# Rotary embedding, eight rows on one core: homes as separate buffers, and one row's load alternating with another's store

## The chip, the cores and the metric

The kernel runs on one core of a Trainium2 chip. The metric is the device time of one execution in microseconds (us). Before the change the median of three runs is 316.32 us (316.31 to 316.72).

## The reference

The input `x` has 8 batch rows of 2048 positions, 16 heads and 64 numbers, all fp32. Each pair of neighbouring numbers is rotated by the angle of its position and of its place in the head:

```python
x_pairs = x.reshape(batch, seq_len, num_heads, head_dim // 2, 2)
x1 = x_pairs[..., 0]
x2 = x_pairs[..., 1]
...
out1 = x1 * cos - x2 * sin
out2 = x1 * sin + x2 * cos
out = np.stack([out1, out2], axis=-1).reshape(batch, seq_len, num_heads, head_dim)
```

`cos` and `sin` have a row of 32 numbers for each position and are the same for all batch rows and heads. 67.1 MB come in and 67.1 MB go out.

## The kernel before

A "row" is one of the eight batch rows, 8.39 MB in fp32. It is laid over the 128 partitions with 16 neighbouring positions on each, so that a partition holds 16 x 1024 = 16384 numbers: 64 KB in fp32 in memory, one contiguous run, and 32 KB in bf16 on chip. Loads that POOL issues convert fp32 to bf16 on their way in, and its stores convert back. A DMA of a whole row is 128 such runs, eight for each of the 16 DMA engines. All loads and stores that POOL issues go through one queue (q0 in the profile) and are taken in the order of issue; SP issues two DMAs through a queue of its own (q1).

There is room for five rows in bf16. The buffer `xt` has five homes, and `HOME` gives row b its home: rows 0 to 4 have homes 0 to 4, and rows 5, 6 and 7 take homes 0, 1 and 2 once rows 0, 1 and 2 are stored.

`rotate(b)` does the work of a row in place with three VectorE (DVE) instructions of 128 x 16384 numbers: L89 multiplies the row by the sine table into `qt`, L92 multiplies the row by the cosine table, and L97 adds `qt`, read with each pair's two numbers swapped. The tables `s_tab` and `c_tab` are built once, the sine with alternating sign (L110 to L112).

The order is written out by hand, and on each engine the instructions run in that order:

- SP loads the first quarter of row 0 in fp32 (`head`, L101) and ACT casts it into its home (L108). POOL issues the loads of the two tables (L102, L103), of the rest of row 0 (L104), of rows 1 and 2 in one DMA, and of rows 3 and 4 in one DMA (`load`, L70).
- DVE builds the tables and rotates row 0 in two parts (4 and 12 positions of 16), then rows 1 to 7.
- `first_store` runs between the first and the second instruction of row 2's rotation. Two one-element copies on ACT, the first of which reads `qt` (L120, L121), hold the store of row 0 (`store`, L74) until that instruction is done.
- Before the store of rows 1 and 2, POOL copies one element of row 4's home into `mark` (L126), so that the store is issued only when rows 3 and 4 have landed.
- Then POOL issues the store of rows 1 and 2 in one DMA, the load of row 5 (which waits for the store of row 0), the load of rows 6 and 7 in one DMA (which waits for the store of rows 1 and 2), the store of rows 3 and 4, and the store of rows 5 and 6, each waiting for its rotations.
- Row 7 leaves in another way. ACT casts it in four parts to fp32 into `wide` (L138), which is the space of homes 3 and 4, and SP stores it (L139).

A DMA is put into its queue when its instruction's waits are over; each DMA posts its completion with a small packet on each engine.

Of the kernel before, what the change touches and what calls it, by code (L numbers as in the profile page):

```python
# [2 lines left out]

# [4 lines left out]


@with_exitstack  # L10
def kernel(
    ctx: ExitStack,
    tc: tile.TileContext,
    x: bass.AP,
    cos: bass.AP,
    sin: bass.AP,
    out: bass.AP,
):
    nc = tc.nc
    fp32 = mybir.dt.float32  # L20
    bf16 = mybir.dt.bfloat16
    mult = mybir.AluOpType.mult
    add = mybir.AluOpType.add

    B, S, H, D = x.shape
    P = 128
    K = S // P
    KP = 16
    D2 = D // 2
    HD = H * D  # L30
    NX = 5
    HEAD = 4
    PART = 4
    STAGE = 3


    HOME = [0, 1, 2, 3, 4, 0, 1, 2]

    x_t = x.rearrange("b (p k) h d -> b p k (h d)", p=P, k=K)
    out_t = out.rearrange("b (p k) h d -> b p k (h d)", p=P, k=K)  # L40
    x_r = x.rearrange("b (p k) h d -> p b (k h d)", p=P, k=K)
    out_r = out.rearrange("b (p k) h d -> p b (k h d)", p=P, k=K)
    cos_t = cos.rearrange("(p k) c -> p (k c)", p=P, k=K)
    sin_t = sin.rearrange("(p k) c -> p (k c)", p=P, k=K)

    consts = ctx.enter_context(tc.tile_pool(name="consts", bufs=1))
    stage = ctx.enter_context(tc.tile_pool(name="stage", bufs=1))

    xt = consts.tile([P, NX, K * HD], bf16)
    cos_sb = consts.tile([P, K * D2], fp32)  # L50
    sin_sb = consts.tile([P, K * D2], fp32)
    c_tab = consts.tile([P, K, D], bf16)
    s_tab = consts.tile([P, K, D], bf16)

    wide = (
        xt[:, STAGE : STAGE + 2]
        .rearrange("p a c -> p (a c)")
        .bitcast(fp32)
        .rearrange("p (k c) -> p k c", c=HD)
    )  # L60

    gate = consts.tile([1, 1], bf16)
    mark = consts.tile([1, 1], bf16)

    def home(b, k0=0, k1=K):
        return xt[:, HOME[b], k0 * HD : k1 * HD].rearrange("p (k c) -> p k c", c=HD)

    def load(b, n):
        h = HOME[b]
        nc.gpsimd.dma_start(out=xt[:, h : h + n], in_=x_r[:, b : b + n])  # L70

    def store(b, n):
        h = HOME[b]
        nc.gpsimd.dma_start(out=out_r[:, b : b + n], in_=xt[:, h : h + n])  # L74

    def rotate(b, k0=0, k1=K, between=None):
        nk = k1 - k0
        xp = home(b, k0, k1)
        qt = stage.tile([P, KP, HD], bf16, name="qt", tag="work")

        def rows(a):
            return a.rearrange("p k (h e) -> p k h e", h=H, e=D)

        def tab(a):
            return dataclasses.replace(
                a, offset=a.offset + k0 * D, ap=[a.ap[0], [D, nk], [0, H], [1, D]]
            )

        nc.vector.tensor_tensor(out=rows(qt[:, :nk]), in0=rows(xp), in1=tab(s_tab), op=mult)  # L89
        if between is not None:  # L90
            between(qt)
        nc.vector.tensor_tensor(out=rows(xp), in0=rows(xp), in1=tab(c_tab), op=mult)  # L92
        q_swap = dataclasses.replace(
            qt, offset=qt.offset + 1, ap=[qt.ap[0], [2, nk * HD // 2], [-1, 2]]
        )
        x3 = xp.rearrange("p k (a j) -> p (k a) j", j=2)
        nc.vector.tensor_tensor(out=x3, in0=x3, in1=q_swap, op=add)  # L97

    with tc.manual_schedule():
        head = stage.tile([P, HEAD, HD], fp32, name="st", tag="work")  # L100
        nc.sync.dma_start(out=head[:, :HEAD], in_=x_t[0, :, :HEAD])  # L101
        nc.gpsimd.dma_start(out=sin_sb, in_=sin_t)  # L102
        nc.gpsimd.dma_start(out=cos_sb, in_=cos_t)  # L103
        nc.gpsimd.dma_start(out=home(0, HEAD), in_=x_t[0, :, HEAD:])  # L104
        load(1, 2)
        load(3, 2)

        nc.scalar.copy(out=home(0, 0, HEAD), in_=head[:, :HEAD])  # L108
        s2 = s_tab.rearrange("p k (i j) -> p (k i) j", j=2)
        nc.vector.tensor_copy(out=s2[:, :, 0], in_=sin_sb)  # L110
        nc.vector.tensor_scalar_mul(s2[:, :, 1], sin_sb, -1.0)  # L111
        nc.vector.tensor_copy(  # L112
            out=c_tab.rearrange("p k (i j) -> p (k i) j", j=2),
            in_=cos_sb.to_broadcast([P, K * D2, 2]),
        )
        rotate(0, 0, HEAD)
        rotate(0, HEAD, K)

        def first_store(qt):
            nc.scalar.copy(out=gate, in_=qt[:1, KP - 1, HD - 1 :])  # L120
            nc.scalar.copy(out=xt[:1, HOME[0], :1], in_=xt[:1, HOME[0], :1])  # L121
            store(0, 1)

        rotate(1)
        rotate(2, between=first_store)
        nc.gpsimd.tensor_copy(out=mark, in_=xt[:1, 4, K * HD - 1 :])  # L126
        store(1, 2)
        load(5, 1)
        load(6, 2)
        rotate(3)  # L130
        rotate(4)
        store(3, 2)
        for b in range(5, B):
            rotate(b)
            if b == 6:
                store(5, 2)
        for k in range(0, K, PART):
            nc.scalar.copy(out=wide[:, k : k + PART], in_=home(B - 1, k, k + PART))  # L138
        nc.sync.dma_start(out=out_t[B - 1], in_=wide)  # L139


# [1 line left out]
_INS = ['x', 'cos', 'sin']  # L143
_OUTS = [((8, 2048, 16, 64), 'float32')]


# [23 lines left out]
```

## Time and profile before

| | us |
|---|---|
| median of the runs | 316.32 |
| the profiled execution's own time | 316.21 |
| its span, first to last instruction | 314.4 |
| DVE busy (30 instructions) | 210.4 |
| DVE idle ahead of L89 | 49.3 |
| ACT busy | 19.3 |
| POOL busy | 12.4 |
| HBM read and written, 67.63 + 67.11 MB | 429 GB/s over the span |

The profile is of one execution. A full row's rotation is three DVE instructions of 8.69 us with gaps of 0.03, 26.15 us together. In the page's second part each digit is the busy share of one of 40 equal slices of the span, in tenths, and its GB/s counts the bytes on the side that is written, so that a load to bf16 counts half of what it reads. DMA times "to landing" run from the issue to the completion. In the chain of waits "another core or an unknown queue" is a wait whose end the profile couldn't put down to an instruction; here these pieces end when a row has landed.

### The profile page before, as it was taken

The numbers are of one execution on the slowest core, as the hardware profiler recorded it, in microseconds if no ns is written. First come the engines' busy times: TensorE is split into PE (matmuls) and PEld (weight loads), VectorE is DVE, ScalarE is ACT, GpSimd is POOL, SyncE is SP. The second block draws the span as 40 slices with busy tenths as digits, with TensorE's granted clock in tenths as the row PEclk, the third lists the DMA queues.
The fourth block names the chain that finished last, engine by engine and source line by source line (L and its number), as shares of the span: only waits on it lengthen the run. The fifth ranks groups of instructions, "written<-read, shape, count | busy, mean of one in ns | idle before, by whom it ended". The sixth has DMA issues, their size and how long they took to land.

```text
span 314.4 us, 114 instructions
## 1 busy us (share of the span) xinstructions
DVE 210.4 (67%) x30; ACT 19.3 (6%) x8; POOL 12.4 (4%) x16
## 2 busy tenths in 40 slices
DVE  0549950099999999999992299903999999200000
ACT  1400000000000000000000000000000000790000
POOL 4000000000002500000000000000000000000000
DMA  7999999999999999999999999999999999999996
GB/s 296 238 267 200 200 200 267 200 200 217 250 200 267 459 475 400 400 492 442 400 200 246 221 200 200 250 217 333 400 525 409 400 400 525 409 400 400 525 409 267
DMA packets 2512, 102.24 MB, mean 325 GB/s; under 512 B 208, under 2 KB 208, under 8 KB 336
## 3 DMA queue, kind: packets, MB, share of 16 engines
q0 software_dynamic: 2224, 91.75, 92.0%
q1 hardware_dynamic: 288, 10.49, 7.9%
HBM read 67.63 MB, written 67.11 MB: 429 GB/s over the span
## 4 chain that ended last, share of the span: by engine, by line
DVE 64%; another core or an unknown queue 13%; DMA 7%; ACT 3%; ACTq 1%; issue 0%; POOL 0%; DVEq 0%; PEldq 0%
DVE qt L89 21%; DVE xt L92 21%; DVE xt L97 21%; DMA xt<-in_x_dram 7%; ACT xt L138 3%; ACTq L165 1%; POOL sin_sb L102 0%; POOL cos_sb L103 0%; DVEq L89 0%; DVEq L92 0%; PEldq L165 0%
## 5 line engine op out<-in xcount | busy, mean ns | idle before, releaser
L89 DVE TENSOR_TENSOR qt<-xt,s_tab 128x16384 bf16<-128x16384 bf16 (+2 forms) x9 | 69.7, 7744 | 49.3 <-DMA xt<-in_x_dram 47.0
L92 DVE TENSOR_TENSOR xt<-xt,c_tab 128x16384 bf16<-128x16384 bf16 (+2 forms) x9 | 69.7, 7743 | 0.4
L97 DVE TENSOR_TENSOR xt<-xt,qt 128x16384 bf16<-128x16384 bf16 (+2 forms) x9 | 69.7, 7744 | 0.3
L138 ACT CAST xt<-xt 128x4096 f32<-128x4096 bf16 x4 | 14.1, 3600 | 171.7 <-DVE xt L97 171.7
L74 POOL DMA_DIRECT2D out_dram<-xt x4 | 2.7, 672 | 184.9 <-ACT xt L121 93.5
L110 DVE CAST s_tab<-sin_sb 128x512 bf16<-128x512 f32 x1 | 0.5, 456 | 8.9 <-DMA sin_sb<-in_sin_dram 8.9
L120 ACT COPY gate<-qt 1x1 bf16<-1x1 bf16 x1 | 0.2, 194 | 85.1 <-DVE qt L89 85.1
L126 POOL COPY mark<-xt 1x1 bf16<-1x1 bf16 x1 | 5.0, 5040 | 2.6 <-DMA xt<-in_x_dram 2.6
L70 POOL DMA_DIRECT2D xt<-in_x_dram x4 | 2.7, 694 | 43.2 <-DMA out_dram<-xt 43.2
L108 ACT CAST xt<-st 128x4096 bf16<-128x4096 f32 x1 | 3.6, 3605 | 6.7 <-DMA st<-in_x_dram 6.7
L108 ACT ACT_TABLE_LOAD x1 | 1.3, 1283 | 0.7 <-PEq L154 0.7
L102 POOL DMA_DIRECT2D sin_sb<-in_sin_dram x1 | 0.7, 696 | 0.8 <-PEq L165 0.8
L112 DVE CAST c_tab<-cos_sb 128x1024 bf16<-128x1024 f32 x1 | 0.7, 685 | 0.0
L103 POOL DMA_DIRECT2D cos_sb<-in_cos_dram x1 | 0.6, 569 | 0.0
L104 POOL DMA_DIRECT2D xt<-in_x_dram x1 | 0.6, 557 | 0.0
L111 DVE TENSOR_SCALAR s_tab<-sin_sb 128x512 bf16<-128x512 f32 x1 | 0.4, 445 | 0.0
L121 ACT COPY xt<-xt 1x1 bf16<-1x1 bf16 x1 | 0.2, 188 | 0.0
L154 POOL MEMSET const-float32-0.0<- 128x1 f32 x1 | 0.1, 99 | 0.2 <-issue 0.2
L154 POOL MEMSET const-bfloat16-1.0<- 128x1 bf16 x1 | 0.1, 103 | 0.0
L154 POOL MEMSET const-float32-1.0<- 128x1 f32 x1 | 0.1, 99 | 0.0
L154 POOL MEMSET const-uint8-127<- 128x1 uint8 x1 | 0.1, 99 | 0.0
## 6 DMA issues: line engine op xcount, KB each, us to landing
xt<-in_x_dram POOLq DMA_DIRECT2D x3, 8192.0 KB, 59.4
xt<-in_x_dram POOLq DMA_DIRECT2D x1, 4096.0 KB, 57.6
xt<-in_x_dram POOLq DMA_DIRECT2D x1, 3072.0 KB, 21.2
st<-in_x_dram SPq DMA_DIRECT2D x1, 2048.0 KB, 8.0
sin_sb<-in_sin_dram POOLq DMA_DIRECT2D x1, 256.0 KB, 7.6
cos_sb<-in_cos_dram POOLq DMA_DIRECT2D x1, 256.0 KB, 7.4
out_dram<-xt POOLq DMA_DIRECT2D x4, 49.8
out_dram<-xt SPq DMA_DIRECT2D x1, 30.0
```

The lines of the kernel that those rows point to most:

```text
L70: nc.gpsimd.dma_start(out=xt[:, h : h + n], in_=x_r[:, b : b + n])
L74: nc.gpsimd.dma_start(out=out_r[:, b : b + n], in_=xt[:, h : h + n])
L89: nc.vector.tensor_tensor(out=rows(qt[:, :nk]), in0=rows(xp), in1=tab(s_tab), op=mult)
L92: nc.vector.tensor_tensor(out=rows(xp), in0=rows(xp), in1=tab(c_tab), op=mult)
L97: nc.vector.tensor_tensor(out=x3, in0=x3, in1=q_swap, op=add)
L102: nc.gpsimd.dma_start(out=sin_sb, in_=sin_t)
L103: nc.gpsimd.dma_start(out=cos_sb, in_=cos_t)
L108: nc.scalar.copy(out=home(0, 0, HEAD), in_=head[:, :HEAD])
L112: nc.vector.tensor_copy(out=c_tab.rearrange("p k (i j) -> p (k i) j", j=2), in_=cos_sb.to_broadcast([P, K * D2, 2]),)
L126: nc.gpsimd.tensor_copy(out=mark, in_=xt[:1, 4, K * HD - 1 :])
L138: nc.scalar.copy(out=wide[:, k : k + PART], in_=home(B - 1, k, k + PART))
L165: with _tile.TileContext(nc) as tc:
```

## The change

The one buffer `xt` becomes four: homes 0, 1 and 2 have one each, and homes 3 and 4 stay together, since `wide` lies over both. `at(b)` gives a row's buffer and its place there. The load of rows 1 and 2 becomes two DMAs, and so do the stores of rows 1 and 2, 3 and 4, and 5 and 6, and the load of rows 6 and 7. The copy into `mark` is left out.

`load` and `store` can take every eighth partition. The load of row 6 and the store of row 3 are each cut into eight DMAs of 16 partitions, g, g + 8, ... g + 120, and POOL issues them in turn: a load, a store, a load, a store. The load of row 7 and the store of row 4 follow. The stores of rows 5 and 6 each come after their own rotation. VectorE, ACT and SP run the same instructions as before, on the new buffers.

```diff
-    xt = consts.tile([P, NX, K * HD], bf16)
+    homes = [consts.tile([P, n, K * HD], bf16, name=f"x{i}") for i, n in enumerate((1, 1, 1, 2))]
...
-        xt[:, STAGE : STAGE + 2]
+        homes[3][:, :2]
...
-    mark = consts.tile([1, 1], bf16)
...
-        return xt[:, HOME[b], k0 * HD : k1 * HD].rearrange("p (k c) -> p k c", c=HD)
+        t, h = at(b)
+        return t[:, h, k0 * HD : k1 * HD].rearrange("p (k c) -> p k c", c=HD)
 
-    def load(b, n):
-        h = HOME[b]
-        nc.gpsimd.dma_start(out=xt[:, h : h + n], in_=x_r[:, b : b + n])
+    def at(b):
+        return homes[min(HOME[b], 3)], max(HOME[b] - 3, 0)
 
-    def store(b, n):
-        h = HOME[b]
-        nc.gpsimd.dma_start(out=out_r[:, b : b + n], in_=xt[:, h : h + n])
+    def load(b, n, g=0, step=1):
+        t, h = at(b)
+        nc.gpsimd.dma_start(out=t[g::step, h : h + n], in_=x_r[g::step, b : b + n])
+
+    def store(b, n, g=0, step=1):
+        t, h = at(b)
+        nc.gpsimd.dma_start(out=out_r[g::step, b : b + n], in_=t[g::step, h : h + n])
...
-        load(1, 2)
+        load(1, 1)
+        load(2, 1)
         load(3, 2)
...
         rotate(1)
         rotate(2, between=first_store)
-        nc.gpsimd.tensor_copy(out=mark, in_=xt[:1, 4, K * HD - 1 :])
-        store(1, 2)
+        store(1, 1)
+        store(2, 1)
         load(5, 1)
-        load(6, 2)
         rotate(3)
         rotate(4)
-        store(3, 2)
+        for g in range(G):
+            load(6, 1, g, G)
+            store(3, 1, g, G)
+        load(7, 1)
+        store(4, 1)
         for b in range(5, B):
             rotate(b)
-            if b == 6:
-                store(5, 2)
+            if b < B - 1:
+                store(b, 1)
```

More of the change, by code (lines that the diff above doesn't have):

```diff
@@ L120, in first_store @@
             nc.scalar.copy(out=gate, in_=qt[:1, KP - 1, HD - 1 :])
-            nc.scalar.copy(out=xt[:1, HOME[0], :1], in_=xt[:1, HOME[0], :1])
+            nc.scalar.copy(out=homes[0][:1, 0, :1], in_=homes[0][:1, 0, :1])
             store(0, 1)
```

3 lines of the change are left out of this document (1 added, 2 removed).

## The prediction

> **What bounds the kernel now.** I read the chain of waits first, because it tempts one to the wrong answer:
>
> ```profile
> DVE 64%; another core or an unknown queue 13%; DMA 7%; ACT 3%; ACTq 1%; issue 0%; POOL 0%; DVEq 0%; PEldq 0%
> ```
>
> VectorE has 64% of the chain, so it looks like the bound. The rows on DMA say otherwise:
>
> ```profile
> DMA  7999999999999999999999999999999999999996
> ...
> q0 software_dynamic: 2224, 91.75, 92.0%
> q1 hardware_dynamic: 288, 10.49, 7.9%
> ```
>
> The two queues' packets fill 99.9% of the time of all 16 DMA engines, and only the first and last of 40 slices are below 9. So the end is the sum of the packets: every store and load stands in one line, and VectorE's idle times are waits for its row's turn in that line. The issues show it again: the last store takes 30 us to land, though a row needs only 19.3 (next paragraph), since it shares the engines with the store of rows 5 and 6.
>
> ```profile
> out_dram<-xt SPq DMA_DIRECT2D x1, 30.0
> ```
>
> The timeline gives the price of a row:
>
> ```profile
> 98.02 0.56 POOL L74 DMA_DIRECT2D out_dram<-xt  x1 [93.53 <-ACT xt L121]
> 101.13 5.04 POOL L126 COPY mark<-xt 1x1 bf16<-1x1 bf16 x1 [2.55 <-DMA xt<-in_x_dram]
> ...
> 120.76 0.58 POOL L70 DMA_DIRECT2D xt<-in_x_dram  x1 [4.90 <-DMA out_dram<-xt]
> ...
> 178.49 8.69 DVE L89 TENSOR_TENSOR qt<-xt,s_tab 128x16384 bf16<-128x16384 bf16 x1 [11.15 <-DMA xt<-in_x_dram]
> ...
> 217.05 8.69 DVE L89 TENSOR_TENSOR qt<-xt,s_tab 128x16384 bf16<-128x16384 bf16 x1 [12.41 <-DMA xt<-in_x_dram]
> ```
>
> Row 5 has landed at 178.5 and rows 6 and 7 at 217.05: 38.6 us for two rows, 16 packets on each engine, 2.412 us a packet. Store 0 runs from 101.1 (loads 3 and 4 landed) to 120.8: 19.6 us for eight packets with POOL's wake-up. Load and store cost the same, 64 KB of fp32 in 2.412 us on each engine (27.2 GB/s), whichever side the fp32 is on.
>
> Does a load overlap a store where they meet now? The DMA view of the stretch from 155 to 163 us, in slices of 0.2 us, counts bytes where packets start:
>
> ```profile
> GB/s 0 0 0 983 2621 1311 328 0 0 0 0 0 0 0 0 0 1639 819 164 0 0 0 0 0 0 0 0 0 1638 819 164 0 0 0 0 0 0 0 0 0
> ```
>
> The last round of store 1-2 starts at 155.77, the first of load 5 at 158.22, the second at 160.63 (first starts, from narrower windows): 4.86 us for a store round and a load round, where two rounds of one kind take 4.825. So nothing is gained at the border, and 0.04 is lost. Read in the same way, load then store (213.73 to 218.56) loses 0.00, load then load across two DMAs (175.11 to 179.95) 0.02, store then store (117.16 to 122.00) 0.02.
>
> **The change, part by part.** Homes as buffers of their own change no size and no DVE instruction (nine rotations, 210.4 us in all).
>
> Load 1-2 in two DMAs: row 1 can be rotated when it lands, at 62.4 - 19.3 = 43.1, not at 62.4; row 0 ends at 43.6, so the idle 18.95 us before row 1 goes and DVE runs some 19 us earlier. Store 0 is then issued near 79. Nothing is gained: the line holds loads until 101, and store 0 still starts there. Should that cover be gone, the 19 us would count. Price: one border load-load, 0.02, and an issue of 0.7 us on POOL behind 90 us of queued loads.
>
> The mark copy goes (5.04 us of POOL). It delayed store 1-2, which stood behind store 0 in the line anyway: 0. Store 1-2 in two DMAs: one border, 0.02; load 5 still waits for store 0, to 120.8, while stores 1 and 2 fill the line to 159.
>
> The interleave. In the program each DMA of the POOL queue takes one of eight semaphores in turn, so from the seventh of the sixteen on each waits for the DMA eight before it, and load 7, store 4, store 5 and store 6 are queued behind these waits on POOL. The first three pairs can be issued from 140 (store 1 landed), the fourth load when store 2 lands (159) and its store when load 5 does (178). From there seven packets, 17 us, always stand ahead of an issue of 0.6 us, so the line doesn't run dry. If that cover were gone, each issue would show about 2.3 us, as between the issue of store 0 (98.02) and its first packet (100.29). The line carries the same bytes, but with a border at each packet: 8 load-store borders at 0.00 and 8 store-load ones (the last before load 7) at 0.04 make 0.32. Store 5 | store 6 adds 0.02; load 7 | store 4 and store 4 | store 5 replace borders that are there now.
>
> Row 6 lands one packet before the interleave's end, about 215 (now 217), row 7 near 236. DVE ends row 7 at 215 + 2 x 26.15 = 267, ACT's four casts (14.1) end at 281, and the last store is issued 2 us earlier than its 283.55. The line is full with stores 4 to 6 until 294, so this is worth 0, and up to some 10 us of delay there would be too.
>
> What the trace doesn't show is a DMA whose 16 rows lie eight partitions apart. If two engines then share a way into SBUF, it must carry 2 x 32 KB in 2.412 us, 27.2 GB/s. Lower end: it does, 0. (A gain is excluded by the engines' own 2.412 us unless load and store overlap, which is a rival.) Upper end: the pair takes turns, 16 x 2.412 = 38.6 us. Nearest row: the head's load, fp32 on both sides, starts 16 KB packets 0.62 us apart, 26.4 GB/s into SBUF; at that rate a pair takes 2.48 us, 16 x 0.068 = 1.1 us more. Part of that is the gap of a small packet, so I take half, 0.55. [...]
>
> Sum: 0.02 + 0.02 + 0.32 + 0.02 = 0.38, with 0.55 it is 0.93. The profiled execution took 316.21 (span 314.4, the rest around it is not touched): 317.14. It lies 0.11 under the median of 316.32, so against the median 317.25; I say 317.2.
>
> **The rivals.** *Overlap (faster).* The change would pay if an engine could read for the next packet while it writes this one. A load and a store together move 96 KB each way, 3.62 us at 27.2 GB/s instead of 4.825; eight pairs save 9.65 us: 316.3 + 0.4 - 9.65 = 307.1. For it: loads fill only the read side, stores only the write side. Against it: the store-load and load-store borders above gained nothing, and those in the interleave are the same event, each with the completion's packet between.
>
> *Eight engines (the change doesn't do what it says).* If packets follow the partition, pairs 0 to 3 fall on eight engines, two packets each, and 4 to 7 on the others. With eight DMAs outstanding the second set starts only when the first load is done: 178.0 + 4.8 + 2.3 = 185.1, 7.1 us late, and ends so: 323.8. For it: eight rows of every whole-row DMA belong to an engine; against it: nothing in the trace.
>
> *Starved issues.* If POOL can build descriptors only between DVE's 8.69 us instructions, then during row 5's rotation (178.5 to 204.6) one DMA gets in at 187.2 and one at 195.9; with the seven standing at 178.0 they last to 199.7, and the next packet comes 2.3 us after 204.6: 7.2 us lost, 323.9. For it: the mark copy was held 5.04 us, to the end of the DVE instruction (106.13). Against it: store 0 was issued at 98.02, inside that same instruction, and ran from 101 on. [...]
>
> *Ways taken in turn*: 316.7 + 38.6 = 355.3. For it: each pair would need all of a way; against it: where engines fall out of step, one loads while the other stores.
>
> **How the numbers follow.** The forecast, borders plus a nearly full way, spans 316.7 (0) to 317.8 (1.1) and gets 0.60; eight engines 0.10, starved issues 0.08, turns 0.07, overlap 0.15. A measurement tells 0.2%, 0.63 us, from no change, so the bound on the slow side is 316.95: of the forecast 0.27 lies under it and 0.33 over it. Slower 0.33 + 0.25 = 0.58, within 0.27, faster 0.15. The range runs from 315.6 (a trace of overlap; 0.13 of it left out) to 324.0 (both 7 us rivals in; turns left out, 0.07).
>
> **What would show it.** Right: both queues still near 100% of the engines; row 1 rotated from 43.6 and store 0 issued near 79; in the stretch from 178 to 217 rounds of packets 2.41 to 2.45 us apart, alternately 32 and 64 KB. Overlap: rounds nearer 1.8 us, row 7 landing near 227. Shared ways: rounds of 2.48 or longer there alone, with longer packets. Eight engines: rounds of eight packets. Starved issues: a gap in the DMA row between 195 and 207. I am wrong altogether if the time moves where the line isn't touched, ahead of 178 or after 236.

## The result, and the profile after

The changed kernel takes 317.59 us (median of 7 runs, 317.27 to 317.82) against 316.32 before (median of 7 runs, 316.27 to 317.29): 1.27 us more. The ratio is 1.0037, with a 95% interval of 1.0027 to 1.0046. The profiled execution took 317.49 us with a span of 315.7, where the one before had 316.21 and 314.4.

From the page of the changed kernel, the DMA row, the queues, and the shares of the chain of waits:

```profile
DMA  7999999999999999999999999999999999999996
...
q0 software_dynamic: 2528, 91.75, 92.1%
q1 hardware_dynamic: 288, 10.49, 7.9%
...
DVE 56%; DMA 24%; ACT 3%; another core or an unknown queue 3%; POOL 1%; ACTq 1%; issue 1%; DVEq 0%; PEldq 0%
```

The two queues fill the 16 engines as before, so the line of packets is still the bound. There are 304 small completion packets more, 19 DMAs of 16. The chain has less of VectorE and more of the load, and this too says nothing of the bound: only the place where DVE waits has moved.

The timeline of the changed kernel at the steps that the prediction named:

```profile
43.45 8.69 DVE L91 TENSOR_TENSOR qt<-x,s_tab 128x16384 bf16<-128x16384 bf16 x1
...
78.94 1.10 POOL L76 DMA_DIRECT2D out_dram<-x  x2 [74.12 <-ACT x L124]
...
121.95 0.53 POOL L72 DMA_DIRECT2D x<-in_x_dram  x1 [25.35 <-DMA out_dram<-x]
...
215.97 8.69 DVE L91 TENSOR_TENSOR qt<-x,s_tab 128x16384 bf16<-128x16384 bf16 x1 [10.43 <-DMA x<-in_x_dram]
...
282.48 0.35 SPq L145 DMA_DIRECT2D out_dram<-x  x1
```

Row 1's rotation and store 0's issue are where they were expected (43.6, near 79). Row 5's load, which waits for store 0, is issued 1.2 us later than before (120.76), and that is ahead of the interleave. So the packets were read in rounds, much as for the prediction. A round is one packet on each of the 16 engines, and it begins here with the first start in it, that of a completion packet ahead of it included. A border is the place where the packets of one DMA follow those of another:

| stretch, in rounds of 16 packets | before, us | after, us | more |
|---|---|---|---|
| start to the first packet of row 1 | 23.02 | 22.92 | -0.10 |
| loads 1 and 2, 16 rounds | 38.63 | 38.65 | 0.02 |
| loads 3 and 4, first 15 rounds | 36.21 | 36.28 | 0.07 |
| loads 3 and 4, last round | 2.41 | 3.36 | 0.95 |
| stores 0 to 2, 24 rounds | 57.91 | 57.93 | 0.02 |
| load 5, 8 rounds | 19.34 | 19.34 | 0.00 |
| next 16 rounds (after: the interleave) | 38.63 | 38.91 | 0.28 |
| last 40 rounds, to the last completion | 96.56 | 96.65 | 0.08 |

The sum is 1.32; the spans differ by 1.3. Two of these lines as the window view has them (length, DVE, ACT and POOL busy, PE clock, DMA share, GB/s on the written side), first before, then after (in the kernel after, the rounds begin 0.04 us later than these windows and have the same length):

```profile
177.52:216.15 38.63, 26.08 (x3) 0.00 (x0) 0.00 (x0) 1.00 1.01 217
97.86:100.27 2.41, 2.41 (x1) 0.00 (x0) 0.56 (x1) 1.00 0.95 204
```

```profile
178.44:217.35 38.91, 27.45 (x4) 0.00 (x0) 6.01 (x12) 1.00 1.01 323
97.81:101.17 3.36, 0.00 (x0) 0.00 (x0) 0.00 (x0) 1.00 1.02 156
```

The 16 rounds of the interleave cost 0.28 us more than 16 rounds of loads. (Their GB/s are higher only because a store's bytes are counted in fp32.) The trace shows what stands at its borders: on each engine a completion packet of 4 bytes, which takes 0.022 us behind a load and 0.042 behind a store that a load follows.

The largest piece, 0.95 us, lies in one round of plain loads, the last before the first store, 77 us ahead of the interleave: the engines are shown busy all through it, and it moves its 0.52 MB at 156 GB/s, where plain loads have 204 to 217. Each of its 16 packets is itself longer, 3.27 to 3.65 us against 2.43 to 2.45 in the kernel before, so this isn't a gap between packets. That piece wasn't in the prediction.

### The profile page after: what moved, and what is told of

It reads as the page before. It is cut to its first block, busy times and chain, and to the rows that moved or that the text cites. A ratio compares the mean times of both kernels' runs of the same rounds, so it can differ in the third digit from the quotient of the medians.

```text
span 315.7 us, 139 instructions
## 1 busy us (share of the span) xinstructions
DVE 210.4 (67%) x30; ACT 19.3 (6%) x8; POOL 15.9 (5%) x34
## 4 chain that ended last, share of the span: by engine, by line
DVE 56%; DMA 24%; ACT 3%; another core or an unknown queue 3%; POOL 1%; ACTq 1%; issue 1%; DVEq 0%; PEldq 0%
DMA x<-in_x_dram 24%; DVE qt L91 19%; DVE x L94 19%; DVE x L99 19%; ACT x L144 3%; ACTq L171 1%; POOL out_dram L76 0%; POOL x L72 0%; POOL sin_sb L104 0%; POOL cos_sb L105 0%; DVEq L91 0%; PEldq L171 0%
## 5 line engine op out<-in xcount | busy, mean ns | idle before, releaser
L91 DVE TENSOR_TENSOR qt<-x,s_tab 128x16384 bf16<-128x16384 bf16 (+2 forms) x9 | 69.7, 7745 | 48.5 <-DMA x<-in_x_dram 46.3
L99 DVE TENSOR_TENSOR x<-x,qt 128x16384 bf16<-128x16384 bf16 (+2 forms) x9 | 69.7, 7743 | 0.3
L94 DVE TENSOR_TENSOR x<-x,c_tab 128x16384 bf16<-128x16384 bf16 (+2 forms) x9 | 69.7, 7743 | 0.3
L144 ACT CAST x<-x 128x4096 f32<-128x4096 bf16 x4 | 14.1, 3602 | 189.7 <-DVE x L99 189.7
L76 POOL DMA_DIRECT2D out_dram<-x x14 | 7.2, 516 | 168.9 <-ACT x L124 74.1
L72 POOL DMA_DIRECT2D x<-in_x_dram x13 | 6.9, 536 | 57.1 <-DMA out_dram<-x 47.0
L111 ACT CAST x<-st 128x4096 bf16<-128x4096 f32 x1 | 3.6, 3605 | 6.5 <-DMA st<-in_x_dram 6.5
L106 POOL DMA_DIRECT2D x<-in_x_dram x1 | 0.6, 556 | 0.0
```

The lines of the kernel that those rows point to most:

```text
L72: nc.gpsimd.dma_start(out=t[g::step, h : h + n], in_=x_r[g::step, b : b + n])
L76: nc.gpsimd.dma_start(out=out_r[g::step, b : b + n], in_=t[g::step, h : h + n])
```

## The experiments

Times are medians; the kernel before, run beside each on the same chip, took 316.28 to 316.42.

**Whole rows again.** To part the interleave from the rest, row 6's load and row 3's store go back to one DMA each.

```diff
-        for g in range(G):
-            load(6, 1, g, G)
-            store(3, 1, g, G)
+        load(6, 1)
+        store(3, 1)
```

> The changed kernel with row 6's load and row 3's store each in one DMA of 128 partitions again, in this order; all else as changed. Theory (the early stores cost about 1.0 us at the first border of loads and stores, near 98 us, and the interleave only its 0.34 us of borders): 317.2, and the round of packets that starts near 97.8 again lasts about 3.4 us. Rival (the interleave is what costs, the long round at 98 us is chance): 316.4.

317.33 us, ratio 1.0028 (1.0017 to 1.0040): 1.02 more than before without any interleave, and the round at 97.82 lasts 3.66 us in its profile. The interleave isn't the main cost.

**Store 0 issued later.** The first of the two ACT copies that hold the store reads the end of row 2's home after its rotation, instead of `qt` after its first instruction.

```diff
-        def first_store(qt):
-            nc.scalar.copy(out=gate, in_=qt[:1, KP - 1, HD - 1 :])
+        def first_store():
+            nc.scalar.copy(out=gate, in_=homes[2][:1, 0, K * HD - 1 :])
...
-        rotate(2, between=first_store)
+        rotate(2)
+        first_store()
```

> The changed kernel with row 0's store held until row 2's rotation is done, so that it is issued near 96 instead of 79 us, 5 us ahead of the first border instead of 22. Theory (a store that stands in the queue long ahead of the border costs): 316.7, and the round at 98 us lasts 2.41 us. Rival one (any store issued ahead of the last load's round costs): 317.6. Rival two (the early stores have nothing to do with it): 317.6 with the long round.

317.43 us, ratio 1.0035 (1.0023 to 1.0047). Store 0 is issued at 96.7, and the packets of the round at 97.86 still take 2.75 to 3.38 us, 3.20 on average. The theory that it takes a long stand in the queue falls: being issued 1.1 us ahead of the last load's round is enough.

**The kernel before with an early store.** One word is moved.

```diff
-        rotate(1)
-        rotate(2, between=first_store)
+        rotate(1, between=first_store)
+        rotate(2)
```

> The kernel before with row 0's store held only by the first instruction of row 1's rotation, so that it is issued near 72 us instead of 98; nothing else is changed, and there is no interleave. Theory (early issue costs): 317.2 to 317.4, with a long round near 98 us. Rival (early issue costs nothing, since the store starts at 101 us in either case): 316.3.

317.25 us, ratio 1.0028 (1.0018 to 1.0039). The early issue alone makes the loss, in the old kernel with its one buffer, its mark and its double loads. The timeline and then the window view of this run:

```profile
71.97 0.55 POOL L74 DMA_DIRECT2D out_dram<-xt  x1 [67.48 <-ACT xt L121]
```

```profile
98.05:101.37 3.32, 3.32 (x1) 0.00 (x0) 0.00 (x0) 1.00 1.00 158
```

The last load round takes 3.32 us, and DVE is busy all through it, so an idle DVE (as in the changed kernel) isn't the reason either.

**The interleave alone.** Rows 1 and 2 share a buffer again, with one load, one store and the mark; row 0's store is issued at 97.9.

```diff
-    homes = [consts.tile([P, n, K * HD], bf16, name=f"x{i}") for i, n in enumerate((1, 1, 1, 2))]
+    homes = [consts.tile([P, n, K * HD], bf16, name=f"x{i}") for i, n in enumerate((1, 2, 2))]
...
-        load(1, 1)
-        load(2, 1)
+        load(1, 2)
...
-        store(1, 1)
-        store(2, 1)
+        nc.gpsimd.tensor_copy(out=mark, in_=homes[2][:1, 1, K * HD - 1 :])
+        store(1, 2)
```

> The changed kernel with rows 1 and 2 in one buffer, loaded in one DMA and stored in one, and the mark copy back: up to row 5's load everything is issued as in the kernel before, and then comes the interleave. Theory (the interleave costs eight borders of 0.04 us): 316.7 (316.32 plus 0.32 for the interleave and 0.02 for one more border), no round longer than 2.46 us between 178 and 220 us. Rival (half of the ways into SBUF, nearly full, cost up to 1.1 us): 317.2 to 317.8, with rounds of 2.48 us.

316.58 us, 0.27 more than before (ratio 1.0006, 0.9998 to 1.0015). That fits the borders, 0.34, and not the 1.1 of a nearly full way.

**The first store moved between the loads.** If the slow round belongs to the first border from loads to stores, it must move with it. The two copies that hold the store, and the mark, are left out.

```diff
         load(1, 2)
-        load(3, 2)
...
+        store(0, 1)
+        load(3, 2)
...
-        rotate(2, between=first_store)
-        nc.gpsimd.tensor_copy(out=mark, in_=xt[:1, 4, K * HD - 1 :])
+        rotate(2)
```

> The kernel before with row 0's store issued between the load of rows 1-2 and that of rows 3-4 (near 44 us, some 18 us ahead of its border), without the two gate copies and the mark; no interleave. Theory one (the first border from loads to stores is slow when its store is already queued): the round of packets ahead of the border at 62 us lasts about 3.4 us, none does near 120 us, and the time is 317.3. Theory two (any such border is slow that has a store queued for long): long rounds at 62 and at 120 us, 318.2. Rival (it hangs on row 4's load or on the time near 98 us): no long round at 62 us, 316.3.

317.43 us, ratio 1.0033 (1.0020 to 1.0045). The DMA view of this run in slices of 0.25 us, from 57 and then from 116 us, shows rounds of loads and then of stores where they start:

```profile
GB/s 1442 131 0 0 0 0 0 0 0 1311 655 131 0 0 0 0 0 0 0 0 0 0 0 262 2884 1049 0 0 0 0 0 0 0 1311 2884 0 0 0 0 0
...
GB/s 918 1180 0 0 0 0 0 0 0 131 1180 786 0 0 0 0 0 0 0 786 2884 524 0 0 0 0 0 0 0 2097 2097 0 0 0 0 0 0 0 524 2621
```

In the first line the last load round starts in the 10th slice and the first store round only 14 slices on (59.30 to 62.96, 3.65 us). In the second line, at the next border from loads to stores, whose store was queued early too, the rounds stay ten slices apart. So the slow round is neither tied to row 4 nor to 98 us, and it comes once.

**A small store first, on SP and on POOL.** Two runs look for what "first" means.

```diff
+        nc.sync.dma_start(out=out_t[0, :KP, 0, : K * D2], in_=sin_sb[:KP])
```

> The changed kernel with a small store added on SP (16 partitions of 2 KB, one for each engine, from the sine table's buffer into output row 0, which row 0's store writes over later), near 9 us. Theory one (what is slow is the core's first write to the output or first read of the chip's memory by a DMA): no long round at 98 us, 316.7 to 316.8. Rival (a store queued behind the loads slows the last of them, whatever has been written earlier): the long round stays, 317.6 to 317.7.

317.76 us, ratio 1.0040 (1.0026 to 1.0054), and the round at 98.22 lasts 3.3 us. An engine's first write to the output isn't it.

```diff
+    first = consts.tile([KP, 512], bf16)
...
+        nc.gpsimd.dma_start(out=out_r[:KP, 0, :512], in_=first)
         load(1, 1)
```

> The changed kernel with a small bf16-to-fp32 store on POOL's queue (16 partitions of 2 KB fp32, zeros that row 0's store writes over) between row 0's load and row 1's. Theory one (the long round belongs to the first store of POOL's queue, once a run): no long round at 98 us, one near 21 to 23 us instead, 317.6. Theory two (it belongs to the first whole-row store behind loads): the long round stays at 98 us, 317.7, and none near 22.

317.67 us, ratio 1.0038 (1.0026 to 1.0051). The DMA view of this run from 95 us:

```profile
GB/s 0 0 1442 524 131 0 0 0 0 0 0 262 1442 393 0 0 0 0 0 0 0 0 0 0 262 1049 2622 262 0 0 0 0 0 0 786 2621 786 0 0 0
```

The last load round starts in the 12th slice and the first store round in the 25th, 3.27 us on: the long round stays, though each engine has carried a store of POOL's queue with the same conversion, of 2 KB.

**One full packet first.** Here an eighth of row 0, one 64 KB packet on each engine, is stored between the loads, and the whole row later.

```diff
         load(2, 1)
-        load(3, 2)
...
         rotate(0, HEAD, K)
+        store(0, 1, 0, G)
+        load(3, 2)
```

> The changed kernel with one sixteenth-partition piece of row 0 (16 partitions, one 64 KB packet for each engine) stored already between the load of row 2 and that of rows 3-4; the whole of row 0 is stored later as before, so that 2.41 us of packets are added: 317.6 + 2.4 = 320.0. Theory (the first full packet that an engine stores is slow to come when it stands ready behind loads, and only that one): a round of 3.4 us ahead of 62 us, none near 101 us. Rival (it takes a whole row's store, or it hangs on the time since the start): no long round at 62 us, one near 103 us.

320.01 us, ratio 1.0107 (1.0089 to 1.0125), with 2.41 us of it in the added packets. The DMA view of this run from 57 and from 98 us:

```profile
GB/s 1573 393 131 0 0 0 0 0 0 131 1704 262 0 0 0 0 0 0 0 0 0 0 0 1049 2359 786 0 0 0 0 0 0 0 787 1049 262 0 0 0 0
...
GB/s 0 0 0 0 655 1180 262 0 0 0 0 0 0 131 1049 918 0 0 0 0 0 0 0 1049 1835 1311 0 0 0 0 0 0 0 1311 2359 524 0 0 0 0
```

The round of loads ahead of the single packet takes 3.36 us (59.49 to 62.85). Ahead of the whole row's store, issued at 79.2 and so again early, the rounds stay 2.41 us apart (the last load round starts at 101.50, the first store round at 103.91). One full packet on each engine is enough to have paid. It isn't shown that its size is what counts: the 2 KB stores also lay in the first 1 MB of the output, and these packets are spread over all of row 0.

**The changed kernel with store 0 at 98.** One element of row 2 is copied on DVE ahead of row 1's rotation, so that DVE waits as it did before the change.

```diff
+    mark = consts.tile([1, 1], bf16)
...
+        nc.vector.tensor_copy(out=mark, in_=homes[2][:1, 0, K * HD - 1 :])
         rotate(1)
```

> The changed kernel with one element of row 2's home copied on DVE ahead of row 1's rotation, so that DVE waits for row 2 as it did before the change and row 0's store is issued near 98 us again; loads, stores and interleave as changed. Theory (of the change's 1.27 us about 0.95 is the early store and the rest borders): 316.7, no round of 3.4 us near 98. Rival (the separate loads or the missing mark cost, not the time of the store's issue): 317.5.

316.59 us, 0.31 more than before (ratio 1.0008, 0.9999 to 1.0017). The timeline and then the window view of this run:

```profile
98.04 1.10 POOL L77 DMA_DIRECT2D out_dram<-x  x2 [93.21 <-ACT x L125]
```

```profile
97.81:100.25 2.44, 2.44 (x1) 0.00 (x0) 1.10 (x2) 1.00 1.00 215
```

The store is issued 0.2 us into the last load's round, and the round takes 2.44. Holding DVE back by 19 us, and with it the store, makes the changed kernel 1.0 us faster.

**Neighbouring partitions.** The interleave of the fourth run, with partitions 16g to 16g + 15 in a DMA.

```diff
-        nc.gpsimd.dma_start(out=t[g::step, h : h + n], in_=x_r[g::step, b : b + n])
+        nc.gpsimd.dma_start(out=t[g : g + step, h : h + n], in_=x_r[g : g + step, b : b + n])
...
-            load(6, 1, g, G)
-            store(3, 1, g, G)
+            load(6, 1, g * KP, KP)
+            store(3, 1, g * KP, KP)
```

> The interleave on the order of the kernel before, as in the earlier run of it (316.58), with each of the sixteen DMAs on 16 neighbouring partitions instead of every eighth. [...] If engines don't share ways, rounds of 2.43 us and 316.6.

331.34 us, ratio 1.0473 (1.0458 to 1.0487). The window view of the interleave in this run:

```profile
177.52:230.60 53.08, 26.60 (x4) 0.00 (x0) 6.00 (x12) 1.00 1.03 246
```

16 rounds take 53.1 us instead of 38.9, 3.32 us each with the engines shown busy all the time. So DMAs of 16 neighbouring partitions take 1.4 times as long, and the change's choice of every eighth partition avoids that. That shared ways into SBUF are the cause is the author's guess and not shown: with the partitions the edit also changes the places in memory, 1 MB in a row for each DMA instead of 16 pieces half a MB apart, and no run parts the two. The trace shows 16 x 16 x 32 KB in 53.08 us, 158 GB/s over both directions; in the first round, which is loads alone, the packets took 3.58 us on average, 146 GB/s.

**The interleave doubled.** On the fourth run, row 7's load and row 4's store alternate too.

```diff
-        load(7, 1)
-        store(4, 1)
+        for g in range(G):
+            load(7, 1, g, G)
+            store(4, 1, g, G)
```

> The interleave on the order of the kernel before (316.58), and row 7's load and row 4's store alternating in the same way too, 8 and 8 DMAs more. Theory (the interleave costs its store-load borders, 0.04 us each): 316.58 + 8 x 0.04 = 316.9. Rival (load and store overlap when they alternate for long, hidden by other losses so far): below 316.3.

344.23 us, ratio 1.0880 (1.0865 to 1.0895), far from both. The window view and the timeline of this run:

```profile
177.78:255.60 77.82, 27.54 (x4) 0.00 (x0) 12.71 (x26) 1.00 1.01 323
```

```profile
254.13 8.69 DVE L93 TENSOR_TENSOR qt<-x,s_tab 128x16384 bf16<-128x16384 bf16 x1 [49.35 <-DMA x<-in_x_dram]
```

The 32 rounds take 77.8 us, 2.43 each, as the border theory has it. But row 6's rotation, whose row was in by 217, starts only when row 7's last piece has landed: in this kernel rows 6 and 7 are in one buffer, and a DMA of every eighth partition seems to count as touching all of it. (In the run with the interleave alone row 7 comes in one DMA into the same buffer, and row 6 is rotated at 215.25.) DVE is then late, the queue runs dry, and 28 us are lost.

**Two interleaves on separate buffers.** On the run with store 0 at 98, row 5's load alternates with row 1's store as well; rows 6 and 7 change homes, and each has a buffer of its own (homes 3 and 4 still share one).

```diff
-    HOME = [0, 1, 2, 3, 4, 0, 1, 2]
+    HOME = [0, 1, 2, 3, 4, 0, 2, 1]
...
-        store(1, 1)
-        store(2, 1)
-        load(5, 1)
+        store(2, 1)
+        for g in range(G):
+            load(5, 1, g, G)
+            store(1, 1, g, G)
```

> The run before this with a second interleave: row 5's load and row 1's store alternate in 8 + 8 DMAs too, behind the store of row 2; rows 6 and 7 change homes for that; every home has a buffer of its own. Theory (store-load borders at 0.04 us each, nothing else): 0.3 us over the run with row 0's store at 98, so 317.0, and all rounds from 140 to 218 us 2.41 to 2.45 us apart. Rival (the interleave as such is what made the doubled one take 344, not a wait on a shared buffer): far above 320.

317.50 us, ratio 1.0038 (1.0024 to 1.0052). The window view of the two interleaves in this run:

```profile
139.15:178.08 38.93, 29.55 (x5) 0.00 (x0) 7.79 (x16) 1.00 1.01 323
178.08:217.01 38.93, 26.08 (x4) 0.00 (x0) 6.01 (x12) 1.00 1.01 323
```

Each takes 0.3 us more than 16 rounds of loads before the change (38.63), and row 6 is rotated at 215.6: no wait on another row's load. The time is still 0.5 over what was expected. In its profile 0.35 us of that are slower rounds of plain loads between 73 and 86 us. Its execution, 317.63, also has 2.2 us outside the span of 315.4, where most others have 1.8; its trace has a packet of 8 KB on the instruction queue at 316.67, after the span's end, as only the doubled run has too (at 344.04). Neither was followed further.

## Why the prediction was right

It said 317.2, slower, and the kernel takes 317.59, slower. The bound and the interleave's border costs were right. Two other terms were wrong and nearly made up for each other: 0.55 us that didn't come, and 0.95 that the prediction didn't have. So it is luck that the sum lies within 0.4 us of the result. A slowdown clear of the noise is due to the 0.95 as well: with a late store the changed kernel is 0.31 us slower, which its interval (0.9999 to 1.0017) doesn't tell from no change.

The prediction named a sign for this: "I am wrong altogether if the time moves where the line isn't touched, ahead of 178 or after 236." Of the 1.32 us in the table, 0.96 lie ahead of 178. By its own sign the account of where the time goes was wrong in its largest part.

- *The bound.* The sum of packets was the right account: every part of the 1.32 us is a length of rounds of packets, and none is a wait of DVE.
- *The borders*, priced at 0.38. The interleave's rounds take 0.28 us more than 16 of loads; with the border to load 7 and the split stores and loads, 0.28 + 0.08 + 0.02 + 0.02 = 0.40. The interleave alone measured 0.27, and the changed kernel with a late store 0.31.
- *The nearly full way*, priced at 0.55: 0. Each of its packets took 2.43 us, loads and stores alike. No run shows the term, a way that two engines share; what the runs showed in its place is these 2.43 us at a step of eight partitions. The lower end, 0, was right, and the nearest row, the head's small packets, was the wrong one to lean on. Sixteen neighbouring partitions, with their places in memory, were slower: 53.1 us for 16 rounds against 38.9.
- *Load 1-2 in two DMAs*, the step that failed: "Nothing is gained: the line holds loads until 101, and store 0 still starts there." Nothing is gained, but store 0 issued at 79 instead of 98 costs 0.95 us in the round ahead of it. The step asked only what an earlier issue could win; the store's place in the line was taken as independent of when it joined.
- *Rivals.* Overlap: a pair of rounds takes 4.87 us in the interleave, where two of one kind take 4.825; nothing overlaps. Eight engines: each round of the interleave starts 16 packets. Starved issues: POOL issued 12 DMAs (6.0 us) within the interleave, most of them under row 5's rotation, and no round was late. Ways taken in turn: no, the rounds took 38.91 us and not twice that.
- *The 2.3 us of an issue.* Two rivals used it, from store 0's issue (98.02) to its first packet (100.29). That is a misreading: the last load's round ran from 97.86 to 100.29, so the store had to wait for it in any case. Where the queue was dry, in the doubled run, a store issued at 280.57 had its first packet at 281.68, 1.1 us later.
- *Positions.* Row 6 at 215.97 (215 said), the last store at 282.48 (281), both shifted by the 0.95.

What the slow round is made of stays open. The runs show when it comes: ahead of the first full-size store packet of each engine, when that store was issued 1.1 us or more before the last load round began (at 44, 72, 79 and 96.7 us), and once a run. It doesn't come when the store is issued within some 0.2 us of that beginning, on either side: in five of six such runs the round's packets took 2.44 or 2.45 us on average. One of the five was issued 0.15 us ahead (97.94 against 98.09, in the doubled run), so that being issued ahead isn't enough. The sixth, the run with the interleave alone (97.88 against 97.92), has packets of 2.44 to 2.84 us, 2.60 on average. Where between 0.15 and 1.1 us the limit lies, no run shows. If a store takes 1.1 us to reach the engines, as in the dry queue, the late ones weren't there yet when the last loads began; that fits and is not tested. Why the load and not the store is slow, and why 2 KB packets don't pay it, the runs don't show. The 31 rounds of plain loads ahead of that round took 0.09 us more in all here than before the change, and 0.13 to 0.39 us more in three runs with a late first store too; that is taken for chance.

## What to carry to other kernels

Where the DMA engines are full from end to end, cost a change in packets and borders, not in waits: cutting and alternating whole-row DMAs cost 0.04 us for each pair of a store and a load, and brought no overlap of loads with stores (4.87 us a pair of rounds, against 4.825 for two of one kind). Issuing a store earlier into a queue that is full anyway cost 0.95 us here; try it alone, and look at the round of packets ahead of it. DMAs of 16 partitions took 38.91 us for 16 rounds when spread over all 128, within 1% of the 38.63 of plain loads, and 53.08, 1.4 times as long, when neighbours (and 1 MB in a row in memory), so spread them; and keep buffers that are filled in strided pieces apart from those that another engine still reads (28 us lost in the doubled run).

## What the runs showed of the hardware

- The first 64 KB store packet on each engine made the load packet ahead of it 0.8 to 1.25 us longer (3.20 to 3.67 us on average, against 2.43) when it was issued 1.1 us or more before that packet's round began, and 0.02 or less in five of six runs where it was issued within 0.2 us of it; a 2 KB store packet ahead of it changed nothing.
- 16 DMAs of one packet per engine ran at 2.43 us a packet, against 2.41 in DMAs of eight or sixteen packets, with some seven ahead of each in the queue (19.2 us from issue to landing for those issued between 178 and 188 us).
- A border between DMAs is a completion packet of 4 bytes on each engine: 0.022 us behind a load, 0.042 behind a store that a load follows. A load and a store in turn take 4.87 us, two loads within a DMA 4.825.
- Sixteen neighbouring partitions, 1 MB in a row in memory, moved at 158 GB/s (on the bf16 side, both directions), sixteen at a step of eight at 216 (16 x 16 x 32 KB in 38.91 us).
